# A hybrid decoder step: residual rows kept in SBUF, stores on ScalarE's queue, another order of work from up to down and at the end

## The chip, the core and the metric

The kernel runs on one core of one Trainium2 chip. TensorE (PE) multiplies, VectorE (DVE), ScalarE (ACT) and GpSimd (POOL) do the elementwise work, and SyncE (SP) issues most of the DMAs. The metric is the device time of one execution in microseconds (us), as the median of several runs.

## What is computed

One layer of a decoder: a norm, one input projection, sliding-window attention beside gated linear attention (GLA), an output projection with a residual add, a second norm, and a SwiGLU feed-forward block with a residual add. There are 1024 prompt rows and 16 meta tokens with model width 1024, and 8 x 8 sample rows; the feed-forward width is 2816, that is 11 pairs of 128 columns. Everything is in float32.

```python
def merge_heads(a, o_gla, og, gla_norm, w_o):
    g = rms_norm(o_gla.astype(a.dtype), gla_norm) * jax.nn.silu(og.reshape(b, t, GLA_HEADS, GLA_DV))
    merged = jnp.concatenate([a, g.reshape(b, t, GLA_V_W)], axis=-1)
    return jnp.einsum('bte,ed->btd', merged, w_o)

def swiglu(h, w_gate, w_up, w_down):
    u = jax.nn.silu(jnp.einsum('btd,df->btf', h, w_gate)) * jnp.einsum('btd,df->btf', h, w_up)
    return jnp.einsum('btf,fd->btd', u, w_down)
...
        x = x + merge_heads(a, o, og, gla_norm[l], w_o[l])
        x = x + swiglu(rms_norm(x, norm2[l]), w_gate[l], w_up[l], w_down[l])
```

## The kernel before

**Number format.** A float32 operand is split into a rounded part "hi" (ACT cast, L1218 or L99) and a rest "lo" (DVE subtract, L1219 or L100). A product is three matmuls, hi by hi, hi by lo and lo by hi (mm3, L105 to L107). For the sample rows the moving operand holds hi and lo side by side, so two matmuls do (mm2, L111 and L112).

**Order of the work.** The order on PE is the program's: generators that yield their estimated cost are interleaved by `merge` (L978), and after that the code is plain loops. ACT, DVE, POOL and SP get their order from a tile scheduler; each of them runs its list strictly in that order, and an instruction that waits holds up everything behind it on the same engine. DMA issues stand in those lists too.

**Up to the second norm.** `merge` at L1092 interleaves the GLA chunks, the attention, the projections and `out0`, which holds out_proj(0) and out_proj(1). out_proj(g) multiplies three row tiles by w_o (L105 to L107, tile `pw`), adds the product to the residual rows `xr` (L1072) and writes them to DRAM as x1d (L1074, on POOL's DMA queue). A second `merge` interleaves out_proj(2) with `norms_a`, which normalises tiles -1 (sample rows) to 3: it loads the rows back from x1d (L1168, on SP), squares and scales them (ACT, L1145 and L1147), turns them on PE (L1155, tile `tp`) and evacuates them (L1157). Only the tiles of the last out_proj stay in SBUF (`x1t`).

**Gate and up.** For each of the 11 pairs p the products with w_gate and w_up are computed with seven block products instead of eight (a Strassen/Winograd form, ORDER = 1, 2, 6, 7, 5, 4, 3). A block product is 24 matmuls of 544 columns in two parts and has a PSUM tile `pf`, of which there are four; the first product of a set is copied out by ACT (L1263), the others are added by DVE (L1265 to L1276). `blocks_A` loads weights on SP, forms block sums on POOL (L1236 to L1239) and splits them into hi_wg, lo_wg, hi_wu, lo_wu. What I call the tail of a pair follows: DVE multiplies up by the silu of gate (L1335), POOL forms block sums (L1346 to L1351), ACT and DVE split the result into `uo`, and SP stores it to DRAM: four small stores usd (L1336) and seven large ones ud (L1343).

**Down.** The pairs are taken in chunks (0), (1, 2), ..., (9, 10). For each chunk the weights are loaded, combined on POOL (L1393 to L1396) and split (`blocks_W`, tiles hi_wd, lo_wd); the sample rows `u8` are loaded and split (u8hl) and multiplied; then for each of four row pairs tp the tile `u` is loaded back from ud (L1406, on SP) and seven products are made into `pd`, of which there are eight PSUM buffers. In the first chunk a product is evacuated into an accumulator Y, by an ACT copy or by a DVE add of the residual, which is loaded again from x1d (L1448, L1450); in later ones DVE adds it (L1470). The last chunk combines the seven accumulators of a row pair while its products arrive (L1474 to L1489, DVE and POOL) and stores the output from SP (L1479, L1490, L1492, L1494).

## Time and profile before

| what | value |
|---|---|
| median of 3 runs | 1297.12 us (1296.54 to 1298.06) |
| the profiled execution: its own time | 1292.29 us |
| its span in the trace | 1290.5 us |
| mean granted TensorE clock | 0.97 of full speed |
| PE busy | 1201.3 us, 93% |
| DVE, ACT, POOL busy | 897.4, 526.8, 412.8 us |

Every time below is from the profiled execution, with 0 at the start of its span. A row of the timeline reads: start, duration, engine, line, operation, output tile <- input tiles, shape, count, and in brackets how long the engine had sat idle before it and what released it. Consecutive instructions of one kind may share a row; its duration then runs from the first start to the last end. "SPq" is the issue of a DMA by SP, not its transfer. A row of the stretches reads: from and to, length, then for PE, weight loads, DVE, ACT and POOL the busy time and the number of instructions, then the granted TensorE clock (1.00 is 2.4 GHz, 0.50 is 1.2 GHz), the share of the DMA engines and GB/s. Matmuls are pipelined, so one that shows 0.39 us is followed by the next after less.

### The profile page before, as it was taken

The page shows a single profiled execution, that of the slowest core. Times are in us where ns is not written, and L with a number is a line of the kernel's source. Part 1 is how long each engine was busy: PE and PEld are TensorE (multiplying, and loading weights), DVE is VectorE, ACT ScalarE, POOL GpSimd, SP SyncE. Part 2 cuts the span into 40 slices and gives each one's busy share as a digit, 9 for nine tenths or more (in the row PEclk, how much of TensorE's full clock was granted, in tenths as well). Part 3 has the DMA queues.
Part 4 walks back from the last instruction along what each step waited for, and adds up shares of the span by engine and source line. Part 5 has one row for each costly group of instructions (what it writes and reads, how often), then busy time and mean ns, then how long its engine had stood idle before and what let it go on. Part 6 is the DMA issues. An engine that isn't in the chain of part 4 may idle for free. (4 is left out here: it accounts for less than half of the span.)

```text
span 1290.5 us, 23115 instructions
## 1 busy us (share of the span) xinstructions
PE 1201.3 (93%) x9106; PEld 1060.6 (82%) x9106; DVE 897.4 (70%) x1758; ACT 526.8 (41%) x938; POOL 412.8 (32%) x354
## 2 busy tenths in 40 slices
PE   6999899999999969799999999999999479999997
PEld 6878787788767857699999999999999458788785
DVE  6747986887599648746665666576657656776687
ACT  5635665664566246523333333343324241221120
POOL 6202202131020111234543454345435422420445
PEclk9989999999999979899999999999999789999999
DMA  6723422243322753215433543354344594665545
GB/s 189 221 76 96 127 79 76 54 120 99 98 82 82 278 200 99 66 51 181 133 117 117 180 133 114 120 176 138 108 125 154 171 357 176 232 246 192 218 175 208
DMA packets 146986, 189.19 MB, mean 147 GB/s; under 512 B 15755, under 2 KB 114990, under 8 KB 146862
## 3 DMA queue, kind: packets, MB, share of 16 engines
q1 hardware_dynamic: 145038, 180.84, 43.1%
q0 software_dynamic: 1840, 6.88, 1.5%
q8 instruction: 71, 1.16, 0.4%
q14 instruction: 37, 0.30, 0.1%
HBM read 136.31 MB, written 52.43 MB: 146 GB/s over the span
## 5 line engine op out<-in xcount | busy, mean ns | idle before, releaser
L105 PE MATMUL pd<-hi_wd,u 128*128 128x512 f32 x308 | 121.9, 396 | 14.0 <-DMA u<-ud 13.8
L106 PE MATMUL pd<-lo_wd,u 128*128 128x512 f32 x308 | 121.6, 395 | 1.5 <-DVE lo_wd L1219 1.5
L107 PE MATMUL pd<-hi_wd,u 128*128 128x512 f32 x308 | 122.0, 396 | 0.0
L1218 ACT CAST hi_wd<-raw_wd 128x1024 fp32r<-128x1024 f32 x44 | 44.9, 1049 | 145.5 <-PE pd L107 75.5
L1470 DVE TENSOR_TENSOR y<-y,pd 128x512 f32<-128x512 f32 x112 | 75.3, 684 | 40.3 <-PE pd L107 40.1
L1218 ACT CAST hi_wg<-raw_wg 128x1024 fp32r<-128x1024 f32 (+1 forms) x44 | 41.5, 943 | 150.7 <-PE pf L106 68.3
L1219 DVE TENSOR_TENSOR uo<-u,uo 128x512 fp32r<-128x512 f32 x77 | 79.6, 1046 | 20.2 <-ACT uo L1218 18.8
L1219 DVE TENSOR_TENSOR lo_wu<-raw_wu,hi_wu 128x1024 fp32r<-128x1024 f32 (+1 forms) x44 | 53.9, 1225 | 47.3 <-ACT hi_wu L1218 47.3
L105 PEld LDWEIGHTS pd<-hi_wd,u 128*128 128x128 f32 x308 | 58.5, 190 | 28.8 <-DMA u<-ud 15.2
L1218 ACT CAST hi_wu<-raw_wu 128x1024 fp32r<-128x1024 f32 (+1 forms) x44 | 41.5, 943 | 79.4 <-POOL raw_wu L1237 28.4
L1219 DVE TENSOR_TENSOR lo_wd<-raw_wd,hi_wd 128x1024 fp32r<-128x1024 f32 x44 | 63.2, 1440 | 12.3 <-ACT hi_wd L1218 12.2
L106 PEld LDWEIGHTS pd<-lo_wd,u 128*128 128x128 f32 x308 | 58.5, 190 | 15.3 <-DVE lo_wd L1219 2.1
L1218 ACT CAST uo<-u 128x512 fp32r<-128x512 f32 x77 | 46.7, 620 | 56.4 <-POOL u L1346 40.1
L107 PEld LDWEIGHTS pd<-hi_wd,u 128*128 128x128 f32 x308 | 58.4, 190 | 12.4
L1219 DVE TENSOR_TENSOR lo_wg<-raw_wg,hi_wg 128x1024 fp32r<-128x1024 f32 (+1 forms) x44 | 49.1, 1116 | 24.9 <-ACT hi_wg L1218 24.9
L1236 POOL TENSOR_TENSOR raw_wg<-raw_wg 128x512 f32<-128x512 f32 x11 | 18.4, 1669 | 142.3 <-DVE lo_wg L1219 142.3
L590 POOL TENSOR_SCALAR sg<-sg 128x512 f32<-128x512 f32 (+1 forms) x9 | 14.1, 1564 | 134.0 <-ACT sg L589 133.9
L1393 POOL TENSOR_TENSOR raw_wd<-raw_wd 128x512 f32<-128x512 f32 x11 | 15.9, 1446 | 126.3 <-DVE lo_wd L1219 121.5
L106 PE MATMUL pw<-lo_wo,hThi 128*128 128x512 f32 x128 | 50.9, 397 | 3.2 <-DVE lo_wo L100 3.2
L105 PE MATMUL pw<-hi_wo,hThi 128*128 128x512 f32 x128 | 52.4, 410 | 0.3 <-DVE xr L1072 0.3
L107 PE MATMUL pw<-hi_wo,hTlo 128*128 128x512 f32 x128 | 50.5, 394 | 0.0
L1236 POOL TENSOR_TENSOR raw_wu<-raw_wu 128x512 f32<-128x512 f32 x11 | 14.2, 1294 | 88.5 <-DVE lo_wu L1219 88.5
(729 smaller groups left out, 4277.1 us busy)
## 6 DMA issues: line engine op xcount, KB each, us to landing
ud<-uo SPq DMA_DIRECT2D x77, 512.0 KB, 3.0
u<-ud SPq DMA_DIRECT2D x44, 896.0 KB, 6.1
raw_wo<-in_w_o_dram SPq DMA_DIRECT2D x24, 512.0 KB, 3.9
raw_wu<-in_w_up_dram SPq DMA_DIRECT2D x22, 512.0 KB, 3.9
raw_wg<-in_w_gate_dram SPq DMA_DIRECT2D x22, 512.0 KB, 4.2
raw_wd<-in_w_down_dram SPq DMA_DIRECT2D x22, 512.0 KB, 5.5
raw_q<-in_w_in_dram SPq DMA_DIRECT2D x12, 512.0 KB, 5.3
raw_gv<-in_w_in_dram SPq DMA_DIRECT2D x12, 512.0 KB, 3.6
```

Source lines behind the costliest of these rows:

```text
L105: nc.tensor.matmul(ps, lh, rh, start=first, stop=False)
L106: nc.tensor.matmul(ps, lh, rl, start=False, stop=False)
L107: nc.tensor.matmul(ps, ll, rh, start=False, stop=last)
L590: nc.gpsimd.tensor_scalar(s, s, 2.0 ** 60, None, op0=ALU.min)
L1218: nc.scalar.copy(hi, src)
L1219: nc.vector.tensor_tensor(lo, src, hi.bitcast(F32), op=ALU.subtract)
L1236: nc.gpsimd.tensor_tensor(a22, a21, a22, op=ALU.add)
L1393: nc.gpsimd.tensor_tensor(b11, b12, b11, op=ALU.subtract)
L1470: tt(a, a, ps, op=ALU.add)
```

## The change

It has three parts.

1. **Residual rows.** `x1t` now keeps every tile, so the second norm reads `xr` in SBUF and normalises it in place; the store to x1d stays, since the residual is read again in down. out_proj(1) moves out of the first merge into the second, where it runs before out_proj(2) (`out12`); norm2 of tiles 4 and 5 is issued earlier.
2. **Gate and up.** The weights of the next pair (for the last pair, the first chunk of down) are requested ahead of the tail, and the tail's eleven stores are issued by ACT instead of SP.
3. **Down.** `blocks_W` serves all pairs of a chunk in turn; the sample rows come after the products of the first chunk, or after the second row pair of later ones. The first chunk is evacuated by plain copies, alternately on ACT and DVE; the residual is added by POOL, one row pair in each of the four middle chunks (`residual`). The products come in the order 1, 2, 3, 7, 5, 6, 4. In the last chunk the accumulators of row pair 3 are combined before its products arrive, so that each product there needs few adds behind it, and the output is stored from ACT's queue.

```diff
             xr.append(x)
-            if g == NG - 1:
-                x1t[t] = x
+            x1t[t] = x
...
         yield from out_proj(0, xpool)
-        yield from out_proj(1, xpool)
...
-            x = x1t.get(t)
-            if x is None:
-                x = pool.tile([P, D], F32, tag="x", name=f"x1_{t}")
-                nc.sync.dma_start(x[0:64 if t < 0 else P], x1_rows(t))
+            x = x1t[t]
...
+    def out12():
+        for g in (1, 2):
+            yield from out_proj(g, npool)
+            traced.append(g)
...
-    merge(norms_a(), out_proj(2, npool))
+    merge(norms_a(), out12())
...
-            nc.sync.dma_start(usd[p][:, i // 2, i % 2, :], cu[i][:, 0:32])
+            nc.scalar.dma_start(usd[p][:, i // 2, i % 2, :], cu[i][:, 0:32])
...
-            nc.sync.dma_start(ud[p][:, :, ORDER.index(m)].rearrange("a p h t -> p a h t"), hl.bitcast(F32))
+            nc.scalar.dma_start(ud[p][:, :, ORDER.index(m)].rearrange("a p h t -> p a h t"), hl.bitcast(F32))
...
+    for p in range(NP):
+        if p:
+            full(A, cg)
+        A = blocks_A(w_up_v, p, "wu")
+        for a in cg:
+            nc.scalar.activation(a, a, AF.Silu)
+        cu = c_tiles(c2pool, "u")
+        full(A, cu)
+        now = cu, cg
+        if p < NP - 1:
+            cg = c_tiles(c1pool, "g")
+            A = blocks_A(w_gate_v, p + 1, "wg")
+        else:
+            W = blocks_W((0,))
+        tail(p, *now)
...
+    def residual(tp):
...
+        ts(y[2], y[2], x1[:, D1], op=ALU.add)
+        ts(y[3], y[3], x1[:, D2], op=ALU.add)
+        ts(y[4], y[4], x2, op=ALU.subtract)
...
+    def finish_combined(tp, m, ps):
...
+        elif m == 4:
+            tt(y[4], y[4], ps, op=ALU.subtract)
+            nc.scalar.dma_start(yp[rows(t2), D1], y[4])
+        elif m == 3:
+            tt(y[3], y[3], ps, op=ALU.add)
+            nc.scalar.dma_start(yp[rows(t1), D2], y[3])
...
+    DOWN = (1, 2, 3, 7, 5, 6, 4)
...
+        if c:
+            W = blocks_W(pairs)
         for tp in range(4):
             U = [load_u(p, tp) for p in pairs]
...
+            for j, m in enumerate(ORDER if last and tp == 3 else DOWN):
...
                 if first:
-
-                    if m == 2:
-                        tt(a, x[0][:, D1], ps, op=ALU.add)
...
+                    if j % 2:
+                        nc.vector.tensor_copy(a, ps)
                     else:
                         nc.scalar.copy(a, ps)
...
+            if c - 1 == tp and not last:
+                residual(tp)
+            if tp == (3 if first else 1):
+                samples(pairs, first, last)
```

How the order moves at the three places that the prediction speaks of:

**PE, last GLA chunk.** Before: `psn` is the state update of the chunk, `pw` the output projection, `tg` the transposes of the normed GLA output `on`; between `psn` and `tg` stand 48 matmuls of `pw`, of which the first three and the last three are shown.

```order
L777 MATMUL po_gla<-S,qG 128x256
L780 MATMUL po_gla<-gv,AT 128x128 x2
L786 MATMUL psn<-gv,kdT 64x128 x4
L105 MATMUL pw_5478<-hi_wo,hThi 128x512
L106 MATMUL pw_5478<-lo_wo,hThi 128x512
L107 MATMUL pw_5478<-hi_wo,hTlo 128x512
...
L105 MATMUL pw_5479<-hi_wo,hThi 128x512
L106 MATMUL pw_5479<-lo_wo,hThi 128x512
L107 MATMUL pw_5479<-hi_wo,hTlo 128x512
L674 MATMUL tg<-ident,on 128x128 x4
```

The same place with the change:

```order
L777 MATMUL po_gla<-S,qG 128x256
L780 MATMUL po_gla<-gv,AT 128x128 x2
L786 MATMUL psn<-gv,kdT 64x128 x4
L674 MATMUL tg<-ident,on 128x128 x4
L105 MATMUL pw_5561<-hi_wo,hThi 128x512
L106 MATMUL pw_5561<-lo_wo,hThi 128x512
L107 MATMUL pw_5561<-hi_wo,hTlo 128x512
```

The 48 matmuls between `psn` and `tg` have moved behind `tg`, into the second merge.

**DVE, end of the up products of a pair.** Before: L1276 is the last add of the up products, L1335 the multiply with silu(gate), `uo` the split of the tail, `lo_wg` the rest part of the next gate weights.

```order
L1276 TENSOR_TENSOR u_10727<-u_10727,pf_10911 128x544
L1219 TENSOR_TENSOR uo<-u_10729,uo 128x4x128
L1335 TENSOR_TENSOR u_10727<-u_10727,g_10512 128x544
L1219 TENSOR_TENSOR lo_wg<-raw_wg,hi_wg 128x1024
L1219 TENSOR_TENSOR uo<-u_10729,uo 128x4x128
```

The same place with the change:

```order
L1279 TENSOR_TENSOR u_10735<-u_10735,pf_10895 128x544
L1222 TENSOR_TENSOR uo<-u_10737,uo 128x4x128
L1222 TENSOR_TENSOR lo_wg<-raw_wg,hi_wg 128x1024
L1333 TENSOR_TENSOR u_10735<-u_10735,g_10456 128x544
L1222 TENSOR_TENSOR uo<-u_10737,uo 128x4x128
```

`lo_wg` now stands ahead of the last multiply.

**SP and ACT, from up to down.** SP before: usd and ud are the stores of the last pair, the loads of `u` for the first chunk of down (L1406) come behind them, each with loads of the residual.

```order
L1343 DMA ud_6164<-uo 128x4x256
L1336 DMA usd_6175<-u_11193 128x32
L1343 DMA ud_6164<-uo 128x4x256 x5
L1406 DMA u<-ud_6154 128x1792
L1448 DMA x_11544<-x1d_108 128x1024
L1450 DMA x1h<-x1d_109 128x512
L1406 DMA u<-ud_6154 128x1792
```

SP with the change:

```order
L83 DMA raw_wu<-in_w_up_dram 128x8x128 x2
L83 DMA raw_wd<-in_w_down_dram 128x1024 x3
L1420 DMA u<-ud_6147 128x1792 x4
L1426 DMA u_11653<-usd_6158 128x128
L83 DMA raw_wd<-in_w_down_dram 128x1024 x3
```

ACT with the change, at the same place (L1555 is the copy of a first-chunk product from PSUM):

```order
L1340 DMA ud_6157<-uo 128x4x256 x2
L1221 CAST uo<-u_11200 128x4x128
L1221 CAST uo<-u_11202 128x4x128
L1340 DMA ud_6157<-uo 128x4x256 x2
L1221 CAST u8hl<-u_11653 128x2x64
L1221 CAST hi_wd<-raw_wd 128x1024 x2
L1555 COPY y_1_11477<-pd 128x512
L1555 COPY y_3_11483<-pd 128x512
```

On SP the four loads of `u` are no longer behind any store; on ACT the first copy out of PSUM is now behind all the casts and stores of the last tail.

## Rows read from the trace of the kernel before

**Rows 1.** The page, part 1: busy time of each engine.

```profile
PE 1201.3 (93%) x9106; PEld 1060.6 (82%) x9106; DVE 897.4 (70%) x1758; ACT 526.8 (41%) x938; POOL 412.8 (32%) x354
```

**Rows 2.** Stretches: before the gate, the steady part, and at the start of down.

```profile
460.00:500.00 40.00, 29.17 (x139) 24.34 (x138) 24.52 (x44) 25.27 (x41) 6.51 (x15) 0.83 0.52 173
...
560.00:1000.00 440.00, 433.87 (x3418) 431.14 (x3417) 286.12 (x337) 153.56 (x214) 200.26 (x123) 1.00 0.44 135
...
1020.00:1040.00 20.00, 8.90 (x28) 7.04 (x28) 7.62 (x9) 4.49 (x9) 3.22 (x2) 0.66 0.83 307
```

**Rows 3.** Timeline, PE: where waits before the gate ended.

```profile
476.57 1.11 PE L1155 MATMUL tp<-ident,x_-1_5759 64*128 64x64 f32 x8 [8.69 <-ACT x_-1_5759 L1147]
...
479.83 3.68 PE L1155 MATMUL tp<-ident,x 128*128 128x128 f32 x16 [2.15 <-ACT x L1147]
...
508.20 0.80 PE L106 MATMUL pw<-lo_wo,hThi 128*128 128x512 f32 x1 [3.15 <-DVE lo_wo L100]
```

**Rows 4.** Timeline, ACT: the first square of the second norm.

```profile
473.25 1.06 ACT L1145 ACTIVATE junk_-1_5761<-x_-1_5759 64x1024 bf16<-64x1024 f32 x1 [8.83 <-DMA x_-1_5759<-x1d-1_107]
```

**Rows 5.** Timeline, DVE: an earlier GLA chunk, from state update to normed output.

```profile
373.65 1.43 DVE L792 SCALAR_TENSOR_TENSOR S<-S,eG,psn 64x128 f32<-64x128 f32 x4
...
375.71 0.68 DVE L666 TENSOR_REDUCE ms<-on 128x4 f32<-128x512 f32 x1
...
378.40 1.13 DVE L669 SCALAR_TENSOR_TENSOR on<-po_gla,r,sg 128x128 f32<-128x128 f32 x4 [1.21 <-POOL r L165]
```

**Rows 6.** Timeline, SP, PE and ACT: one pair of the steady part.

```profile
927.95 0.37 SPq L1343 DMA_DIRECT2D ud<-uo  x1
...
930.98 0.40 PE L107 MATMUL pf<-T2hia,lo_wg 128*128 128x288 f32 x1 [0.54 <-DVE lo_wg L1219]
...
932.63 0.61 ACT L1263 COPY g<-pf 128x544 f32<-128x544 f32 x1
...
936.87 0.30 PE L105 MATMUL pf<-T1hia,hi_wg 128*128 128x288 f32 x1
```

**Rows 7.** Timeline, PE: the waits between up and the first chunk of down.

```profile
1016.60 0.77 PE L111 MATMUL pd<-hi_wd,u8hl 128*128 128x512 f32 x1 [6.12 <-DVE u8hl L1219]
...
1031.22 0.79 PE L105 MATMUL pd<-hi_wd,u 128*128 128x512 f32 x1 [11.10 <-DMA u<-ud]
```

**Rows 8.** Timeline, POOL, ACT and SP: the tail of the last pair.

```profile
1019.43 2.12 POOL L1351 TENSOR_TENSOR u<-u,u 128x512 f32<-128x512 f32 x1
...
1021.58 0.62 ACT L1218 CAST uo<-u 128x512 fp32r<-128x512 f32 x1 [1.58 <-POOL u L1351]
...
1023.79 0.97 SPq L1343 DMA_DIRECT2D ud<-uo  x2
...
1024.86 0.99 SPq L1406 DMA_DIRECT2D u<-ud  x1
```

**Rows 9.** Timeline, PE: the waits for the sample rows of the second chunk.

```profile
1058.54 0.80 PE L111 MATMUL pd<-hi_wd,u8hl 128*128 128x512 f32 x1 [5.24 <-DVE u8hl L1219]
...
1064.27 0.80 PE L111 MATMUL pd<-hi_wd,u8hl 128*128 128x512 f32 x1 [3.65 <-DVE u8hl L1219]
```

**Rows 10.** Timeline, PE and SP: the last chunk, to the last store.

```profile
1263.78 0.50 PE L105 MATMUL pd<-hi_wd,u 128*128 128x512 f32 x1 [1.50 <-DMA u<-ud]
...
1274.89 0.51 PE L105 MATMUL pd<-hi_wd,u 128*128 128x512 f32 x1 [1.21 <-DMA u<-ud]
...
1283.72 0.40 PE L107 MATMUL pd<-hi_wd,u 128*128 128x512 f32 x1
...
1287.11 0.41 SPq L1494 DMA_DIRECT2D out_dram<-y  x1
```

**Rows 11.** The page, parts 5 and 6: splits, accumulations and transfers of down.

```profile
L1218 ACT CAST hi_wd<-raw_wd 128x1024 fp32r<-128x1024 f32 x44 | 44.9, 1049 | 145.5 <-PE pd L107 75.5
L1470 DVE TENSOR_TENSOR y<-y,pd 128x512 f32<-128x512 f32 x112 | 75.3, 684 | 40.3 <-PE pd L107 40.1
...
u<-ud SPq DMA_DIRECT2D x44, 896.0 KB, 6.1
```

More of the change, by code (lines that the diff above doesn't have):

```diff
@@ L1127, in hymba_step @@
     c1pool_, c1pool = open_pool("c1", 5, "right")
-    npool_, npool = open_pool("n", 4, "right")
-    napool_, napool = open_pool("na", 4)
+    npool_, npool = open_pool("n", 6, "right")
     def h2_part(m, sl, src):
@@ L1291, in norms_b @@
     def norms_b():
-        xt = [normed2(tp, npool) for tp in (2, 3)]
+        norm2(5, x1t[5], npool)
+        xt = [[(t, x1t[t]) for t in (4, 5)], normed2(3, npool)]
         yield 0.0, 4.0
@@ L1323, in full, with tail @@
             combine(t, slice(0, NH), m, ps[2])
-    for p in range(NP):
-        if p:
-            cg = c_tiles(c1pool, "g")
-            full(blocks_A(w_gate_v, p, "wg"), cg)
-        for a in cg:
-            nc.scalar.activation(a, a, AF.Silu)
-        cu = c_tiles(c2pool, "u")
-        full(blocks_A(w_up_v, p, "wu"), cu)
+    def tail(p, cu, cg):
         tt, ts = nc.vector.tensor_tensor, nc.gpsimd.tensor_tensor
@@ L1352, in hymba_step, with blocks_W, put @@
         put(6, a11), put(3, a12)
+    def blocks_W(pairs):
+        W = [{} for p in pairs]
+        raws = [[load_raw([w_down_v[:, f:f + 1, :]], 1, D, "wd") for f in (2 * p, 2 * p + 1)] for p in pairs]
+        def put(i, j, n):
+            for B, raw in zip(W, raws):
+                hl = parts("wd")
+                split_into(*hl, raw[n])
+                for c, m in enumerate((i, j)):
+                    B[m] = tuple(a[:, c * 512:c * 512 + 512] for a in hl)
+        put(1, 0, 0)
+        put(2, 3, 1)
+        for raw in raws:
+            (b11, b12), (b21, b22) = (halves(r) for r in raw)
+            nc.gpsimd.tensor_tensor(b11, b12, b11, op=ALU.subtract)
+            nc.gpsimd.tensor_tensor(b12, b22, b12, op=ALU.subtract)
+            nc.gpsimd.tensor_tensor(b22, b22, b11, op=ALU.subtract)
+            nc.gpsimd.tensor_tensor(b21, b22, b21, op=ALU.subtract)
+        put(5, 7, 0)
+        put(4, 6, 1)
+        return W
+    for p in range(NP):
[13 more added lines that the diff above has]
+        tail(p, *now)
     psp_.__exit__(None, None, None)
@@ L1368, in hymba_step @@
     wpool.append(w2)
+    nsplit[0] = 4
     upool = last_pool("u", 4, "right")
@@ L1417, in hymba_step, with rows, samples @@
     CHUNKS = [(0,)] + [(p, p + 1) for p in range(1, NP, 2)]
-    tt = nc.vector.tensor_tensor
-    for pairs in CHUNKS:
-        first, last = pairs is CHUNKS[0], pairs is CHUNKS[-1]
-        W = [blocks_W(p) for p in pairs]
+    tt, ts = nc.vector.tensor_tensor, nc.gpsimd.tensor_tensor
+    def rows(t):
+        return slice(t * P, t * P + P)
+    def samples(pairs, first, last):
         US = [load_u8(p) for p in pairs]
-        if first:
-            x8 = xpool2.tile([P, D], F32, tag="x", name="x8")
-            nc.sync.dma_start(x8[0:64], x1_rows(-1))
         for half, blocks in ((D1, (1, 2)), (D2, (0, 3))):
@@ L1432, in hymba_step @@
             if first:
-                tt(Y8[0:64, half], x8[0:64, half], ps[0:64], op=ALU.add)
-                nc.scalar.copy(Y8[64:128, half], ps[64:128])
+                nc.scalar.copy(Y8[:, half], ps)
             else:
@@ new lines, in finish @@
+    def finish(tp, x22, m, ps):
+        y = Y[tp]
+        t1, t2 = 2 * tp, 2 * tp + 1
+        a = y[m]
+        if m != 4:
+            tt(a, a, ps, op=ALU.add)
+        if m == 2:
+            ts(a, a, y[1], op=ALU.add)
+            nc.scalar.dma_start(yp[rows(t1), D1], a)
+        elif m == 7:
+            ts(x22, x22, a, op=ALU.add)
+            ts(y[4], a, y[4], op=ALU.subtract)
+        elif m == 6:
+            tt(a, a, y[1], op=ALU.add)
+            tt(y[1], a, y[5], op=ALU.add)
+            ts(x22, x22, y[1], op=ALU.add)
+            nc.scalar.dma_start(yp[rows(t2), D2], x22)
+            tt(y[3], y[3], y[1], op=ALU.add)
+            nc.scalar.dma_start(yp[rows(t1), D2], y[3])
+        elif m == 4:
+            tt(a, a, ps, op=ALU.subtract)
+            tt(a, a, y[6], op=ALU.add)
+            nc.scalar.dma_start(yp[rows(t2), D1], a)
@@ L1442, in hymba_step @@
+    DOWN = (1, 2, 3, 7, 5, 6, 4)
+    NC = len(CHUNKS)
+    for c, pairs in enumerate(CHUNKS):
+        first, last = c == 0, c == NC - 1
+        if c:
+            W = blocks_W(pairs)
         for tp in range(4):
             U = [load_u(p, tp) for p in pairs]
-            y = Y[tp]
-            t1, t2 = 2 * tp, 2 * tp + 1
-            if first:
-                x = [xpool2.tile([P, D], F32, tag="x", name="x1")]
-                nc.sync.dma_start(x[0], x1_rows(t1))
-                x.append(xpool2.tile([P, 512], F32, tag="xh", name="x1h"))
-                nc.sync.dma_start(x[1], x1_rows(t2)[:, D1])
```

115 lines of the change are left out of this document (56 added, 59 removed).

## The prediction, as put on record before the run

> **What bounds the kernel now.** I read the page first: PE is busy for 1201.3 of 1290.5 us [rows 1], so no change of order can take off more than about 89 us, and only where PE stands still or runs slowly. The view of stretches shows where that is. From 560 to 1000 PE is busy for 433.87 of 440 us at full clock; from 460 to 500 for only 29.17 of 40 us, and from 1020 to 1040 for 8.90 of 20 us with a granted clock of 0.66, that is, partly at 1.2 GHz [rows 2]. Then I read PE's timeline for its idle brackets. Three groups stand out: before the gate 8.69, 2.15 and 3.15 us [rows 3], from up to down 6.12 and 11.10 [rows 7] and again 5.24 and 3.65 [rows 9], and at the end 1.50 and 1.21 [rows 10]. In the steady part there is one wait of 0.54 us a pair for lo_wg [rows 6]; ten pairs have it. The change touches all four places, so I cost it place by place, by what PE waits for there now and will wait for next.
>
> **The price of a matmul.** From 1274.89 to 1283.72 PE starts 38 matmuls after the wait for the second tile `u` (row pair 3 has 42, and three come before it) [rows 10]: 0.232 us each, so a single-pair product of three is 0.70 and the first chunk with its 28 products 19.5 us. After a long wait they go slower. The eight sample matmuls from 1016.60 until the next wait begins (1031.22 - 11.10 = 1020.12) take 3.52 us [rows 7] instead of 1.86, a loss of 1.7. The first chunk takes from 1031.22 to 1058.54 - 5.24 = 1053.30 [rows 7, 9], 22.1 us instead of 19.5, a loss of 2.6. Those are my prices for a restart of PE.
>
> **Place 1, before the gate.** The reload of x1 goes, and with it the 8.83 us for which ACT's first square waits on that DMA [rows 4], seen on PE as 8.69 and then 2.15. The 3.15 for lo_wo should go too, since its split is no longer late behind the norm. With a restart of 1.8 (between 1.7 and 2.6, by the shorter wait) that is 15.8 us. What is late next: in the last GLA chunk the 48 matmuls between `psn` and `tg` no longer cover the chain that makes `on`. In an earlier chunk that chain runs on DVE from the state update at 373.65 to the last multiply at 378.40 + 1.13 [rows 5], 5.9 us with other work of up to 0.7 in it. I take 5.4 as PE's new wait. Then three row tiles are normed on ACT before PE can turn the third: one square and one scale more than is covered, about 1.06 each by the square's row [rows 4], 2.2 together. The second long wait again costs a restart, 2.2. Sum of the new: 9.8. **Gain 6.** Bounds: 0, if the third tile's norm and the restart are twice that dear, and 12, if PE's remaining `pw` cover the norms and there is no second restart.
>
> **Place 2, the steady part.** On DVE lo_wg moves ahead of one multiply of about 0.7 us (the DVE add of the same kind is 0.68 [rows 11]), so the 0.54 can vanish ten times: 5.4 us. Against that ACT issues eleven stores a pair, 0.37 us each by SP's row [rows 6], 4.1 us of a pair of 43.2 us. By its total ACT has room: it is busy for 153.56 of 440 us [rows 2]. But an issue waits for DVE's split, and what is queued behind it on ACT is the copy of g that frees the first of four `pf` tiles. That copy now ends at 932.63 + 0.61 = 933.24, and PE's fifth product starts at 936.87 [rows 6], a slack of 3.6 us. Behind two more casts of 0.62 [rows 8] and two or three issues with their waits I place its end between 934.7 and 936.4. It still makes it, narrowly, so I take **a gain of 3**, with bounds of 5.4 and, if each pair loses 0.5 net, -5. The earlier requests for weights cost nothing: SP's stores that stood among them are gone.
>
> **Place 3, from up to down.** The sample rows and the loads of `u` cause all four waits: 6.12 + 11.10 + 5.24 + 3.65 = 26.1 us [rows 7, 9]. The load of `u` is issued at 1024.86 because it stands on SP behind the last stores, whose final issue ends at 1023.79 + 0.97; that store waits for POOL's block sum, which ends at 1021.55, and for the splits behind it [rows 8]. With the change the loads stand before any of this, and the sample rows come after the products. With the restarts 1.7 and 2.6, and for the second pair of waits 1.15 (1058.54 to 1060.62 for four matmuls) and an estimate of 1.5, the full worth is 33 us. What is late next: PE can now run the first chunk from 1010.5 on, but has eight `pd` buffers. Eight products end at about 1016.1. The ninth needs the first copy by ACT, which stands behind the whole last tail: the last cast `uo` ends at 1022.2 [rows 8], the last two issues after DVE's splits at about 1024.8, and then come a small cast and two of 1.05 [rows 11], so the copy ends at about 1027.5. PE waits 11 us and pays a restart of 2. ACT then serves products and weight splits in turn, and the raw weights of the second chunk arrive late as their buffers come free; I take 2 for that. **Gain 33 - 11 - 2 - 2 = 18.** Bounds: 31, if ACT does not hold PE up, and 10, if a whole load (6.1 by that of `u` [rows 11]) and a POOL sum of about 2 [rows 8] stand uncovered ahead of the second chunk, 8 more.
>
> **The middle chunks.** The residual is added by three POOL instructions a chunk, at most 2.12 each by the nearest POOL row [rows 8], in a stretch of some 38 us; the next accumulation into the same tiles comes a chunk later. The cover is POOL's idle two thirds [rows 1]; if it were gone, 3 x 2.1 us in four chunks would be at stake. I count nothing.
>
> **Place 4, the end.** The loads of `u` no longer stand behind output stores on SP, so 1.50 + 1.21 = 2.7 go. The last matmul ends at 1283.72 + 0.40 = 1284.1 and the span at 1290.5, 6.4 us later, of which 1290.5 - 1287.52 = 3.0 follow the last issue [rows 10]. With the change one add of 0.68 [rows 11], one issue of 0.41 and the 3.0 follow: 4.1. **Gain 2.7 + 2.3 = 5**, bounds 2 and 6.
>
> **The sum.** 6 + 3 + 18 + 5 = 32 us off the profiled execution's 1292.3: 1260.3. The median of the runs stands 4.8 above that execution, so I forecast **1265 us**.
>
> **Rivals.**
>
> *ACT is in time at the start of down.* If the tail's stores and casts are spread early enough, the ninth product does not wait, and place 3 is worth 31: a sum of 45, 1247.3 + 4.8 = **1252**. For it: ACT is busy only a third of the time [rows 2]. Against it: the last cast of the tail cannot start before POOL's sum at 1021.55 [rows 8], and the first copy stands behind it. Chance 0.18.
>
> *The transfers, not their place in the queue, set when `u` arrives.* From 1020 to 1040 the DMA engines already move 307 GB/s at a share of 0.83 [rows 2]. If stores on ACT's queue, weight loads and the `u` loads share them so that PE's first product still starts near 1031, place 3 is worth the 5.24 and 3.65 with their restarts and little else, 11, and place 4 keeps its two waits, worth 2. The sum is then 6 + 3 + 11 + 2 = 22: 1270.3 + 4.8 = **1275**. Against it: the load stands behind a waiting store in time, not in bandwidth; it is issued right after that store [rows 8]. Chance 0.12. The Trainium skill, in "DMA: Bandwidth & Descriptors", section "Issuing engines are not separate DMA queues", states the rule behind this rival: starting DMAs on several engines saves only the sequencer's time for the start, since all run on the same engines. By that rule alone the move of the stores would be worth their issue time. The trace disagrees for this place, with SP's issues waiting until 1024.76 for POOL and DVE.
>
> *ACT holds up every pair (slower).* If the copy of g slips not to 936.4 but past 940.2, that is by 3.6 + 3.3 us from where it ends now, PE loses 3.3 us in each of ten pairs, 33 in all. The other places give 29, so the time is 1292.3 + 4 + 4.8 = **1301**. The price per pair from which this decides is 3.2 us, since under that the sum is still a gain within the measurement. For it: the stores' waits for DVE lie on the engine that frees PSUM. Against it: ACT's busy third. Chance 0.05.
>
> *Nothing comes of it:* the gains of places 1 and 3 are given back in full, by waits of the same length; chance 0.03.
>
> **Chances and range.** The forecast has 0.62, the rivals 0.18, 0.12, 0.05 and 0.03. About 0.2% of the time, 2.6 us, is what a measurement can tell from no change. Faster by more: 0.62 + 0.18 + 0.12 = 0.92; same 0.03; slower 0.05. The forecast's own range, by the bounds of place 3 and half those of the others, is 1253 to 1277. The range for 8 in 10 takes in the first two rivals with their own spread: 1247 to 1286.
>
> **What would show it.** Right: no wait for a DMA of x1 on ACT before the gate, but one of 4 to 7 us on PE for `tg` or `on`; no 0.54 waits for lo_wg; PE's first product of down near 1010 on the old clock, then, eight products later, one wait of 8 to 13 us that ends with ACT's first copy of y; no waits of several us for u8hl; 3 to 5 us from the last matmul to the end. Wrong: a wait on PE for a `pf` tile in every pair; a first product of down that waits for `u`; or a second chunk that waits more than 4 us for its weights.

## The result and the profile after

| | before | changed |
|---|---|---|
| median of the runs | 1296.83 us (4 runs) | 1278.10 us (4 runs) |
| ratio, 95% interval | | 0.986 [0.9843, 0.9878] |
| profiled execution, its span | 1292.29, 1290.5 us | 1279.4, 1277.6 us |

The change made the kernel 1.4% faster, 18.7 us by the medians; the forecast was 1265, the range 1247 to 1286. The two profiled executions are only 12.9 us apart, because that of before lies below its other runs and that of the change above its own. The working was made against profiled executions, so it is held against those 12.9. (In the experiments below the median of the kernel before is 1292 to 1294 us, so the 18.7 may be some 2 to 5 us too many.)

The page and the stretches of the changed kernel, to be read beside [rows 1, 2]:

```profile
PE 1197.0 (94%) x9106; PEld 1058.5 (83%) x9106; DVE 887.7 (69%) x1756; ACT 525.5 (41%) x939; POOL 433.3 (34%) x371
```

```profile
460.00:500.00 40.00, 38.37 (x170) 31.82 (x171) 24.86 (x30) 21.45 (x27) 4.10 (x9) 0.96 0.49 172
560.00:1000.00 440.00, 436.49 (x3431) 433.11 (x3431) 282.37 (x337) 151.80 (x214) 192.78 (x123) 1.00 0.44 136
1020.00:1040.00 20.00, 6.30 (x13) 4.11 (x14) 9.13 (x12) 8.20 (x13) 7.99 (x6) 0.50 0.89 318
```

PE is now busy for 38.37 of the 40 us from 460 to 500, where it was 29.17. From 1020 to 1040 it is busy for less than before, 6.30 against 8.90 us, at a granted clock of 0.50, that is at 1.2 GHz for the whole stretch.

Because the absolute times shift, I cut each trace at five points of PE's timeline: the last `psn`, the first gate product, the first up product, the last up product, the last matmul, and the end of the span. The lengths of these stages, worked out from the starts of those matmuls, are the table in which all kernels of this study stand:

| kernel | psn to gate | to first up | gate and up | to last matmul | to the end | ratio to before [95%] |
|---|---|---|---|---|---|---|
| before | 87.9 | 38.5 | 454.0 | 273.5 | 6.8 | |
| changed | 82.9 | 42.0 | 452.4 | 255.9 | 13.4 | 0.9860 [0.9843, 0.9878] |
| e1 tail stores on SP | 81.5 | 41.7 | 447.7 | 252.2 | 13.5 | 0.9801 [0.9774, 0.9828] |
| e2 samples early | 81.4 | 42.0 | 452.2 | 258.3 | 11.6 | 0.9862 [0.9836, 0.9889] |
| e3 last tail on DVE | 82.8 | 43.4 | 452.1 | 255.3 | 13.5 | 0.9881 [0.9853, 0.9909] |
| e4 x1 store on SP | 82.9 | 38.7 | 450.5 | 254.9 | 13.3 | 0.9832 [0.9803, 0.9860] |
| e5 last stores on ACT | 81.4 | 41.8 | 447.7 | 255.8 | 13.4 | 0.9836 [0.9812, 0.9860] |
| e6 old finish | 82.7 | 42.4 | 451.0 | 265.8 | 9.6 | 0.9889 [0.9865, 0.9913] |
| e7 no residency | 88.6 | 38.7 | 451.9 | 256.2 | 13.1 | 0.9885 [0.9859, 0.9910] |
| e8 combined | 82.6 | 36.5 | 447.7 | 258.5 | 9.5 | 0.9773 [0.9748, 0.9798] |
| e9 combine ahead | 82.6 | 42.1 | 453.0 | 269.3 | 4.8 | 0.9896 [0.9875, 0.9916] |
| e10 u ahead | 82.9 | 42.1 | 447.7 | 249.3 | 13.4 | 0.9787 [0.9767, 0.9808] |
| e11 best | 82.8 | 36.6 | 447.7 | 262.8 | 4.7 | 0.9765 [0.9742, 0.9789] |
| e12 combine one | 82.1 | 37.8 | 447.7 | 253.1 | 6.9 | 0.9737 [0.9713, 0.9761] |

Before against changed: +5.0, -3.5, +1.6, +17.6 and -6.6 us, together 14.2 before rounding. The part ahead of `psn`, which the change does not touch, was 1.3 longer; in the study's traces it lies between 426.7 and 431.1 us. That makes the 12.9. (Untouched stages also differ by a few tenths to 1.5 us between kernels; I read nothing from such differences.)

Where PE waits now, from its timeline (start, duration, what; in brackets the idle time and what ended it):

```profile
437.35 1.16 PE L674 MATMUL tg<-ident,on 128*128 128x128 f32 x4 [5.66 <-DVE on L669]
...
528.29 1.94 PE L1150 MATMUL tp<-ident,xr 128*128 128x128 f32 x8 [7.04 <-DVE xr L1152]
...
606.82 0.40 PE L107 MATMUL pf<-T2hia,lo_wu 128*128 128x288 f32 x1 [0.73 <-DVE lo_wu L1222]
...
1029.49 0.79 PE L105 MATMUL pd<-hi_wd,u 128*128 128x512 f32 x1 [14.74 <-ACT y L1555]
...
1033.65 0.79 PE L105 MATMUL pd<-hi_wd,u 128*128 128x512 f32 x1 [2.51 <-DVE y L1553]
...
1036.99 0.80 PE L105 MATMUL pd<-hi_wd,u 128*128 128x512 f32 x1 [1.70 <-ACT y L1555]
```

These answer to [rows 3, 6, 7, 9, 10]. The reload is gone, and in its place stand the chain of the GLA output (5.66) and a wait of 7.04 inside the gate. The 0.54 for lo_wg is gone, and in six of the ten pairs after the first there is one of 0.18 to 0.73 for lo_wu, which makes 2.8 us. Down starts without a wait for `u`, makes eight products, and then waits 14.74 us for ACT's first copy. After 1037 there is no wait over 0.6 us left, none for u8hl and none for `u` at the end.

ACT, SP and DVE from up to down, which answer to [rows 8]:

```profile
1007.12 1.27 SPq L1420 DMA_DIRECT2D u<-ud  x3
...
1014.68 0.62 ACT L1221 CAST uo<-u 128x512 fp32r<-128x512 f32 x1 [4.77 <-POOL u L1343]
...
1018.98 0.62 ACT L1221 CAST uo<-u 128x512 fp32r<-128x512 f32 x1 [3.68 <-DMA ud<-uo]
...
1023.79 0.62 ACT L1221 CAST uo<-u 128x512 fp32r<-128x512 f32 x1 [2.36 <-DMA ud<-uo]
1023.81 1.71 ACTq L1340 DMA_DIRECT2D ud<-uo  x2
...
1028.86 0.58 ACT L1555 COPY y<-pd 128x512 f32<-128x512 f32 x1
...
1032.90 1.89 DVE L1553 COPY y<-pd 128x512 f32<-128x512 f32 x3 [3.64 <-DMA ud<-uo]
...
1036.35 2.05 ACT L1555 COPY y<-pd 128x512 f32<-128x512 f32 x4 [6.92 <-DMA ud<-uo]
```

The loads of `u` go out at 1007, as the order promised. But twice a cast of the last tail waits for a landed store, since there are three `uo` buffers, and the copy that PE needs stands behind all of it. The next copies out of PSUM wait for landed stores again; the last store of `uo` goes out at 1025.16 and lands at 1036.28. A copy does not read `uo`, so it must be the accumulator it writes that is not free: the source closes the pool of `uo` before it allocates the accumulators, and I infer that they share memory. These waits are PE's 2.51 and 1.70.

The last chunk, DVE, POOL, PE and ACT, which answers to the second half of [rows 10]:

```profile
1256.57 5.67 DVE L1483 TENSOR_TENSOR y<-y,y 128x512 f32<-128x512 f32 x1
...
1261.65 1.74 POOL L1481 TENSOR_TENSOR y<-y,y 128x512 f32<-128x512 f32 x1
...
1263.43 0.69 DVE L1490 TENSOR_TENSOR y<-y,pd 128x512 f32<-128x512 f32 x1 [1.19 <-POOL y L1481]
...
1264.18 0.40 PE L107 MATMUL pd<-hi_wd,u 128*128 128x512 f32 x1
...
1266.91 0.67 DVE L1511 TENSOR_TENSOR y<-y,pd 128x512 f32<-128x512 f32 x1
...
1274.32 0.34 ACTq L1531 DMA_DIRECT2D out_dram<-y  x1
```

PE's last matmul starts at 1264.18, but DVE only begins on the first product of row pair 3 (L1511) at 1266.91. All seven are then waiting in PSUM, and the end is DVE's and POOL's: 13.4 us against 6.8 before.

### The profile page after: what moved, and what is told of

Read it like the earlier page. It is cut to its first block, busy times and chain, and to the rows that moved or that the text cites. A ratio compares the mean times of both kernels' runs of the same rounds, so it can differ in the third digit from the quotient of the medians.

```text
span 1277.6 us, 23094 instructions
## 1 busy us (share of the span) xinstructions
PE 1197.0 (94%) x9106; PEld 1058.5 (83%) x9106; DVE 887.7 (69%) x1756; ACT 525.5 (41%) x939; POOL 433.3 (34%) x371
## 3 DMA queue, kind: packets, MB, share of 16 engines
q10 hardware_dynamic: 49376, 45.56, 11.1%
## 4 chain that ended last, share of the span: by engine, by line
PE 36%; issue 25%; POOL 17%; DVE 13%; ACT 4%; DMA 4%; POOLq 0%; SPq 0%; DVEq 0%; ACTq 0%
PE pd L105 4%; PE pd L106 4%; PE pd L107 4%; DMA ud<-uo 2%; POOL raw_wu L1242 2%; ACT hi_wg L1221 2%; POOL raw_wg L1240 1%; POOL raw_wg L1239 1%; PE gv L105 1%; PE gv L107 1%; PE gv L106 1%; POOL u L1348 1%; POOL u L1346 1%; PE q L105 1%; PE q L107 1%
## 5 line engine op out<-in xcount | busy, mean ns | idle before, releaser
L1222 DVE TENSOR_TENSOR lo_wu<-raw_wu,hi_wu 128x1024 fp32r<-128x1024 f32 (+1 forms) x44 | 49.2, 1118 | 55.5 <-ACT hi_wu L1221 55.5
L105 PEld LDWEIGHTS pd<-hi_wd,u 128*128 128x128 f32 x308 | 58.4, 190 | 34.0 <-ACT y L1555 17.6
L106 PEld LDWEIGHTS pd<-lo_wd,u 128*128 128x128 f32 x308 | 58.5, 190 | 13.5 <-DVE lo_wd L1222 0.8
L1369 POOL TENSOR_TENSOR raw_wd<-raw_wd 128x512 f32<-128x512 f32 x11 | 18.9, 1717 | 70.7 <-DVE lo_wd L1222 70.7
```

The source lines that it names most:

```text
L105: nc.tensor.matmul(ps, lh, rh, start=first, stop=False)
L106: nc.tensor.matmul(ps, lh, rl, start=False, stop=False)
L1222: nc.vector.tensor_tensor(lo, src, hi.bitcast(F32), op=ALU.subtract)
L1369: nc.gpsimd.tensor_tensor(b22, b22, b11, op=ALU.subtract)
```

## The experiments

All were timed in five rounds against the kernel before, whose median was 1292 to 1294 us in these; so the ratios are what is compared. That median was 1296.83 us in the runs beside the changed kernel, a difference of 0.004, so a ratio nearer than that to the changed kernel's 0.9860 (e2 to e7 and e9) says little by itself; there the stages decide. e1 to e7 and e9 change one thing of the changed kernel; e8 and e10 to e12 join several.

**e1: the tail's stores back on SP.**

```diff
-            nc.scalar.dma_start(usd[p][:, i // 2, i % 2, :], cu[i][:, 0:32])
+            nc.sync.dma_start(usd[p][:, i // 2, i % 2, :], cu[i][:, 0:32])
...
-            nc.scalar.dma_start(ud[p][:, :, ORDER.index(m)].rearrange("a p h t -> p a h t"), hl.bitcast(F32))
+            nc.sync.dma_start(ud[p][:, :, ORDER.index(m)].rearrange("a p h t -> p a h t"), hl.bitcast(F32))
```

> Undoes one part: the tail's eleven stores a pair are issued by SP again, all else as in the changed kernel. In SP's list one load of u for the first chunk then stands ahead of the last six stores, three behind them. Theory (a waiting issue on ACT holds up what stands behind it): the waits for lo_wu at the up products, six pairs of ten with 0.28 to 0.73 us, 3.3 in all, go; the first ACT copy of down comes 1 to 3 us earlier than 1028.86, and PE's first wait in down ends at 1026 to 1031, now by the late loads of u. Sum -4 to +2 us. Rival (the place of the loads behind the stores is the whole worth of the part): PE's second row pair waits for u until after 1031 and the kernel is 5 us or more slower.

Measured: 0.9801, below the changed kernel's interval, 7.6 us faster by the ratios, where -4 to +2 was expected. Gate and up take 447.7 us instead of 452.4, flat over all pairs; the waits for lo_wu are gone but for the one at the first pair. The stage to the last matmul is 3.7 shorter, although PE now waits for `u`. The timeline of ACT, SP and PE in e1:

```profile
1011.60 0.62 ACT L1221 CAST uo<-u 128x512 fp32r<-128x512 f32 x1 [2.72 <-POOL u L1348]
1012.12 0.58 ACT L1555 COPY y<-pd 128x512 f32<-128x512 f32 x1
...
1013.42 1.99 SPq L1420 DMA_DIRECT2D u<-ud  x3
...
1019.65 0.79 PE L105 MATMUL pd<-hi_wd,u 128*128 128x512 f32 x1 [13.80 <-DMA u<-ud]
```

The last up product starts at 997.93 in this run, so the first copy comes 14.2 us after it, where it took 1028.86 - 1008.24 = 20.6 with the stores on ACT. So the expected gain was too small: moving the stores to ACT's queue cost more than it gave. The rival, 5 us or more slower, falls.

**e5: only the last pair's stores on ACT.** The two lines of e1, with `nc.sync if p < NP - 1 else nc.scalar`.

> The stores of the pairs 0 to 9 go back to SP, those of the last pair stay on ACT. Theory (two separate losses on ACT's queue: one in every pair, one from up to down): the stretch of gate and up shrinks as it did with all stores on SP, 452.4 to about 447.7 us, and the start of down stays as in the changed kernel with a wait of some 14 us for ACT's first copy and 255 us from the last up product to the last matmul; in all 4 to 5 us faster than the changed kernel, 3 to 4 slower than with all stores on SP. Rival (the place of the last stores decides nothing): as fast as with all stores on SP, within 1.5 us.

Measured: 0.9836; gate and up 447.7 as in e1, to the last matmul 255.8 as in the changed kernel, with waits of 14.38 and 4.58 us. There are two losses and they are separate, 4.7 in the pairs and 3.6 from up to down; the gain on the changed kernel, some 3 us, is a little less than the 4 to 5 expected.

**e3: the last tail's block sums on DVE.** `ts = tt if p == NP - 1 else nc.gpsimd.tensor_tensor`.

> For the last pair alone the four block sums of the tail run on DVE instead of POOL. Theory (the first copy out of PSUM is late because the tail's chain POOL, ACT, DVE, store is long): the four sums take 4 x 0.7 instead of 5.7 us, the wait of 14.74 us on PE at the start of down shrinks by 3 to 5, and so does the time. Rival (the casts wait for landed stores of uo, of which there are three buffers): the wait shrinks by less than 1.5 us.

Measured: 0.9881, no gain; the waits are 14.29 and 4.73. POOL's sums are not what the copy waits for, so the rival stands: the casts wait for landed stores, 4.39 and 2.52 us in this trace.

**e4: the x1d stores of out_proj(2) on SP.**

```diff
-            nc.gpsimd.dma_start(x1_rows(t), xr[i][0:64 if t < 0 else P])
+            (nc.sync if g == 2 else nc.gpsimd).dma_start(x1_rows(t), xr[i][0:64 if t < 0 else P])
```

> The x1d stores of out_proj(2) are issued by SP instead of POOL, where they stand behind block sums. Theory (normalising in place has to wait until the store of the same tile has landed): ACT's wait of 4.57 us for x1d ahead of the scaling goes to under 1, PE's wait of 7.04 us at 521 falls to 2 to 4, the time by 3 to 5. Rival (the chain square, POOL's root, scaling is the bound there): PE waits 6 to 7 us as before, under 1 us in the time.

Measured: 0.9832, and the stage from the first gate to the first up product falls from 42.0 to 38.7. In the changed kernel ACT's scaling waits for the store of the tile that it overwrites. Behind it on ACT stands a copy of g, behind that copy on DVE an add and then the evacuation of `tp`, and for that PE waits:

```profile
524.03 1.15 ACT L1142 ACTIVATE xr<-xr,r 128x1024 f32<-128x1024 f32 x1 [4.57 <-DMA x1d<-xr]
```

With the stores on SP that wait is gone from ACT and PE's 7.04 has become 2.34:

```profile
521.88 1.15 ACT L1142 ACTIVATE xr<-xr,r 128x1024 f32<-128x1024 f32 x1 [0.66 <-POOL r L165]
523.01 1.16 PE L1150 MATMUL tp<-ident,xr 128*128 128x128 f32 x8 [2.34 <-DVE xr L1152]
```

**e7: part 1 undone,** with the code of the kernel before for it.

> Undoes part 1: out_proj(1) back in the first merge, tiles -1 to 4 loaded again from DRAM ahead of the second norm, as in the kernel before; the rest as changed. Theory (part 1 took 10.8 us of waits for the reload away and gave most of it back to the wait for the GLA chain, 5.7 us, and to the third tile's norm behind its own store, 7.0): the time rises by only 1 to 3 us. Rival (part 1 is worth the 6 us that the prediction gave it): it rises by 5 to 7.

Measured: 0.9885. The first two stages take 127.3 instead of 124.8 us, with PE's old waits back (9.29, 2.15 and 2.97). Part 1 is worth 2.5 us by the traces, as the theory said; by the ratios the two kernels' intervals overlap.

**e2: the samples of the last chunk earlier.** `if tp == (3 if first else 0 if last else 1)`.

> In the last chunk the sample rows come after row pair 0 instead of 1, so POOL's two sums for them (2.4 us each) leave the stretch ahead of the finish of row pair 2. Theory (POOL's order at the end is what makes DVE late): the 13.4 us from the last matmul to the end of the span become 8 to 10, the kernel 3 to 5 us faster. Rival (DVE has too much to do in the last chunk, whatever the order): under 1 us.

Measured: 0.9862, no change. The end is 1.8 shorter and the stage ahead of it 2.4 longer. The place of POOL's sample sums in the chunk is not the cause.

**e6: the old finish for row pairs 0 to 2,** with the code of the kernel before in `finish` and ORDER in the whole last chunk.

> In the last chunk row pairs 0 to 2 are finished as in the kernel before (product order 1, 2, 6, 7, 5, 4, 3, its adds and its POOL sums); row pair 3 and the queues stay as changed. The number of adds is the same. Theory (with the new order the add that frees a PSUM buffer stands on DVE behind POOL's sums of the same row pair, and DVE falls behind PE): the 13.4 us from the last matmul to the end fall to 5 to 8, the time by 5 to 8. Rival (DVE has simply too many adds in this chunk, whatever their order): 11 to 14 us remain.

Measured: 0.9889. The end falls to 9.6, but the last matmul comes 9.9 later. The theory about the order falls: in this place the old finish is no better. Of the delay 5.9 us lie in the last chunk, which takes 48.9 us instead of 43.0, with waits of 2.83 and 0.68 us for hi_wd and lo_wd at its head and a granted clock of 0.81 from 1230 to 1240. Most of the rest lies in the four chunks before, which the edit does not touch: without a wait each takes 42.9 us instead of 42.1, and why is not shown.

**e8: e1, e4 and e6 together.**

> A candidate better than both kernels: the changed kernel with the tail's stores on SP, the x1d stores of out_proj(2) on SP, and the old finish of row pairs 0 to 2 in the last chunk. If the three gains are separate they add: 7.6 for the tail's stores, 3.6 for the x1d stores and 5 to 8 for the end, 16 to 19 us faster than the changed kernel, a ratio to the kernel before of 0.971 to 0.974. If the end is bound by DVE whatever the order: 11, a ratio of 0.977.

Measured: 0.9773, the value named for an end that DVE bounds. The end is 4.0 us shorter than in e1 and the stage ahead of it 6.3 longer, so the gain is that of e1 and e4, and the finish adds nothing.

**e9: all row pairs combined in the fifth chunk.** The last chunk uses ORDER and `finish_combined` for every row pair.

```diff
+            if c == NC - 2:
+                x22 = xpool2.tile([P, 512], F32, tag="xh", name="x22")
+                nc.sync.dma_start(x22, x1_rows(2 * tp + 1)[:, D2])
+                combined(tp, x22)
```

> The accumulators of all four row pairs are combined in the fifth chunk, not those of row pair 3 alone in the last: three adds of two SBUF tiles on DVE and one POOL sum of each of row pairs 0 to 2 leave the last chunk, and every add of DVE that is left there reads PSUM. Theory (in the last chunk DVE's adds of two SBUF tiles, 0.7 us alone and 1.2 to 5.7 beside POOL, and its waits for POOL make it fall behind PE): the 13.4 us from the last matmul to the end become 4 to 6, the last matmul comes at most 2 later, the time falls by 6 to 9. Rival (the added work in the fifth chunk holds up PE there by as much): within 2.

Measured: 0.9896, and by the stages 4.8 us slower than the changed kernel. The end does become short, 4.8 us, now that every product's add of DVE in the last chunk reads PSUM; but the edit moves sums of POOL as well, so which of the two makes it short stays open. What it costs is that the sums hold up the last chunk's weights, as PE's timeline of e9 shows:

```profile
1227.51 0.59 PE L105 MATMUL pd<-hi_wd,u 128*128 128x512 f32 x1 [4.34 <-ACT hi_wd L1221]
...
1230.87 0.79 PE L106 MATMUL pd<-lo_wd,u 128*128 128x512 f32 x1 [2.76 <-DVE lo_wd L1222]
```

With two more of 0.99 and 0.89 that is 9.0 us, and the clock in the stretch from 1220 to 1240 is 0.74. ACT's casts hi_wd wait there for POOL's sums of the weights, and POOL runs without a pause from 1212.21 to 1238. The theory was right for the end alone: the last matmul comes 13.4 us later, not 2. The rival named the right cost and put it too low, since the loss is larger than the gain.

**e10: `u` ahead of the stores.** e1, and

```diff
+        dma = nc.scalar if (p, tp) == (0, 1) else nc.sync
-        nc.sync.dma_start(u.bitcast(F32), ud[p][tp])
+        dma.dma_start(u.bitcast(F32), ud[p][tp])
```

> As with all tail stores on SP, and the load of u of the first chunk's second row pair is issued by ACT, so that in SP's list three loads of u stand ahead of the last six large stores. Theory (with the stores on SP the start of down waits for u alone, since ACT's first copy is done by 1012.7 on that run's clock and u lands at 1019.6): the wait of 13.8 us falls to 7 to 9, the time by 4 to 6 against that run, a ratio to before of about 0.976. Rival (the loads take the DMA engines from the last stores, whose buffers the tail waits for): the wait ends with ACT's copy and stays above 11.

Measured: 0.9787; the wait falls from 13.80 to 7.34 us and the stage by 2.9. The wait now ends with ACT's copy, as the rival said, though well under 11 us, and PE's first product waits 3.08 us for hi_wd, where in e1 it waited 2.58 for `u`. By the ratio it can't be told from e1.

**e11: e1, e4, e9 and e10 together.**

> The changes that helped together: tail stores and the x1d stores of out_proj(2) on SP, the loads of u ahead, all row pairs combined in the fifth chunk. If they add up: 7.6 + 3.6 + 5 + 7 = 23 us faster than the changed kernel, a ratio to before of 0.968. If the end or the start of down is bound elsewhere: 0.973 to 0.978.

Measured: 0.9765: short end (4.7), late weights (8.5 us of waits at the head of the last chunk), as in e9.

**e12: as e11, but only row pair 0 combined ahead;** row pairs 1 and 2 as changed, row pair 3 in the last chunk.

> Tail stores and x1d stores of out_proj(2) on SP, u ahead, and only row pair 0 is combined in the fifth chunk; row pairs 1 and 2 are finished as in the changed kernel, row pair 3 combined in the last chunk. Theory (POOL and DVE have room for one row pair's sums in the fifth chunk, where four held up the last weights by 9 us): PE's waits at the head of the last chunk stay under 2 us, the end after the last matmul falls from 13.4 to 8 to 11, ratio to before 0.972 to 0.975. Rival (each row pair combined ahead costs as much there as it saves at the end): ratio 0.976 to 0.979, as with the kernels on these parts alone.

Measured: 0.9737 [0.9713, 0.9761], 1259.08 us beside 1292.37 before: faster than both kernels. The head of the last chunk costs one wait, more than the 2 us expected, and the end is shorter than expected, 6.9:

```profile
1208.56 0.79 PE L105 MATMUL pd<-hi_wd,u 128*128 128x512 f32 x1 [2.82 <-ACT hi_wd L1221]
...
1250.43 0.40 PE L107 MATMUL pd<-hi_wd,u 128*128 128x512 f32 x1
...
1254.22 0.34 ACTq L1532 DMA_DIRECT2D out_dram<-y  x1
```

The short end is not the gain. The last chunk takes 48.6 us here and 43.1 in e10, so the chunk and the end together take 55.5 against 56.5: by these traces combining row pair 0 ahead is worth about 1 us, and most of what leaves the end comes back ahead of the last matmul, as the rival said. The rest is e1, e4 and e10 joined, which was not run without the combining.

## Why the prediction was right or wrong

The sign and the range of 1247 to 1286 were right, and so was what PE waits for first in the main stage. The sum of 32 us was not: by the stages it is 14.2. The median of 1278.10 lies just outside the forecast's own range of 1253 to 1277, and as a number the second rival's 1275 came nearer, though not by its mechanism. Every place gave less than was forecast, and that the miss is not larger is luck: 5.1 us came from the middle chunks, which the prediction counted at nothing.

**Place 1, forecast 6, measured 1.6,** that is 5.0 ahead of the gate and -3.5 inside the first gate. The reload's waits went, and the chain that makes `on` cost 5.66 against the 5.4 worked out. Ahead of the gate PE waited for no norm, and 1.97 of the 3.15 for lo_wo stayed. The step that failed is "three row tiles are normed on ACT before PE can turn the third ... 2.2 together": it ends at the gate, has no term for the norms inside it, and no thought for the store. A tile that is normalised in place can't be overwritten until its x1d store has landed, and those stores stand on POOL among the block sums of the first gate weights. The wait was 7.04 us on PE, in the gate, and e4 shows that the store was the cause of 4.7 of it. It was there before too, as 1.06 us on ACT. I had looked at what the change adds, not at what the moved work now stands next to.

**Place 2, forecast 3, measured 1.6.** The 0.54 for lo_wg went, as the order said, and the copy of g did make it. The loss came elsewhere, in the split of the up weights, for which the working has no term. One pair of the changed kernel:

```profile
588.64 2.07 ACTq L1340 DMA_DIRECT2D ud<-uo  x2
590.80 0.62 ACT L1221 CAST uo<-u 128x512 fp32r<-128x512 f32 x1 [1.58 <-DVE uo L1222]
592.54 0.62 ACT L1221 CAST uo<-u 128x512 fp32r<-128x512 f32 x1 [1.11 <-DMA ud<-uo]
...
593.06 1.05 ACT L1221 CAST hi_wu<-raw_wu 128x1024 fp32r<-128x1024 f32 x1
...
598.14 1.29 POOL L1239 TENSOR_TENSOR raw_wu<-raw_wu 128x512 f32<-128x512 f32 x1 [6.67 <-DVE lo_wu L1222]
...
599.60 0.30 PE L105 MATMUL pf<-B11hia,hi_wu 128*128 128x288 f32 x1
...
600.83 1.05 ACT L1221 CAST hi_wu<-raw_wu 128x1024 fp32r<-128x1024 f32 x1 [2.68 <-POOL raw_wu L1240]
```

The same pair of e1, with the stores on SP:

```profile
582.98 1.05 ACT L1221 CAST hi_wu<-raw_wu 128x1024 fp32r<-128x1024 f32 x1
...
591.51 1.29 POOL L1239 TENSOR_TENSOR raw_wu<-raw_wu 128x512 f32<-128x512 f32 x1 [5.69 <-DVE lo_wu L1222]
...
593.96 0.30 PE L105 MATMUL pf<-B11hia,hi_wu 128*128 128x288 f32 x1
...
594.21 1.05 ACT L1221 CAST hi_wu<-raw_wu 128x1024 fp32r<-128x1024 f32 x1 [2.69 <-POOL raw_wu L1240]
```

With the stores on ACT the first hi_wu is cast 6.5 us ahead of the first up product (599.60 - 593.06), with the stores on SP 11.0 us ahead (593.96 - 582.98): in ACT's list it stands behind two more casts of the tail and behind issues that wait for DVE's splits. From there the delay runs on through DVE's lo_wu and POOL's sum to the cast at 600.83, for which ACT itself is idle. That cast starts 1.23 us after the first up product, in e1 0.25, and PE then waits 0.73 us for lo_wu. The ten up products after the first take up to 22.2 us each in the changed kernel, 21.2 in e1; that is the whole loss. With the stores on SP the part is worth 6.3 us; the move to ACT's queue took 4.7 of it. The slower rival had the right kind of mechanism, on another tile and a seventh of its size.

**Place 3, forecast 18, measured 10.3.** The stage of 17.6 us in the table holds more than this place. From the last up product to the end of the second chunk, and from there to the last chunk, first before, then changed:

```profile
1010.20:1107.06 96.86, 70.75 (x279) 56.32 (x278) 61.39 (x73) 30.57 (x45) 26.51 (x18) 0.84 0.72 260
1107.06:1238.54 131.48, 128.06 (x553) 103.27 (x552) 93.67 (x120) 25.61 (x30) 39.67 (x27) 1.00 0.57 210
```

```profile
1008.24:1094.78 86.54, 67.18 (x279) 53.32 (x278) 54.90 (x70) 29.62 (x46) 33.08 (x24) 0.88 0.72 251
1094.78:1221.13 126.35, 126.35 (x553) 103.67 (x552) 91.00 (x120) 25.84 (x29) 47.22 (x31) 1.00 0.64 236
```

Eight products, then a wait for ACT's first copy: that was the forecast, with 11 us. It was 14.74. I let the last cast follow POOL's sum, as in [rows 8]; with the change it waits for landed stores of `uo`, 3.68 and 2.36 us, and e3, which shortens POOL's part, gains nothing. In this stretch the loads of `u` and the weights share the DMA engines with those stores (share 0.89). The two terms of 2 us behind it were too small as well. At the pace of the three chunks that follow (126.35 us for the 552 matmuls that start there) the first two chunks need 63.2 us. Before, 33.7 us stood on top of that, as the prediction had it; with the change 23.4 do, where it took 11 + 2 + 2. They are the 14.74, the 2.51 and 1.70 for the next copies, and some 4.4 of slow matmuls and one short wait. The second chunk's weights, for which 2 us were set aside, were in time.

**The middle chunks, forecast 0, measured 5.1.** The residual cost PE nothing, as counted: in the third to fifth chunk it is busy for all of the 126.35 us. But before it had waited there for lo_wd, 0.76 us at 1115.97, 1.70 at 1196.52 and 0.76 at 1203.63, with slower matmuls after, and these waits went. Which part of the change removed them no run shows.

**Place 4, forecast +5, measured -4.5,** that is 2.1 in the last chunk and -6.6 behind it. The 2.7 for `u` went. The step that failed is "With the change one add of 0.68, one issue of 0.41 and the 3.0 follow": it takes for granted that DVE is level with PE at the last matmul. It was not. I had counted the adds behind the last matmul and not DVE's and POOL's work in the whole last chunk, where eight PSUM buffers let PE run on while DVE falls behind. From the first matmul of the last chunk to the end of the span, before and changed:

```profile
1238.54:1290.52 51.98, 42.86 (x185) 34.21 (x183) 41.79 (x51) 2.10 (x2) 26.51 (x18) 0.99 0.58 202
```

```profile
1221.13:1277.62 56.49, 42.83 (x185) 34.22 (x183) 45.08 (x52) 2.69 (x3) 40.25 (x25) 0.92 0.54 191
```

DVE has one instruction more, POOL seven: two sums of the residual that run over from the chunk before, two for the sample rows, and seven instead of four for row pair 3. DVE's adds of two SBUF tiles wait while POOL sums, as the last section shows. e2 and e6 show that the order inside the chunk is not the point; e9 shows that combining the accumulators ahead of the chunk brings the end to 4.8, near the 4.1 that the prediction worked out, and moves the cost to the weights ahead of it. By the last chunk and the end together no kernel gets back to the 52.0 us of before: it is 56.5 changed, 59.9 in e9 and 55.5 in e12. Which of POOL's sums costs how much no run separates.

**The rivals.** ACT was not in time, so the 1252 did not come. Of the transfers: in the changed kernel PE's first product did not wait for `u`, so that rival's mechanism fell for `u`. Something like it shows for the stores: they landed late behind the loads that now stand ahead of them (the last section), and the casts and copies waited for them. And the rule that stood beside it deserves more than I gave it. The Trainium skill ("DMA: Bandwidth & Descriptors", "Issuing engines are not separate DMA queues") says that starting DMAs on more engines saves only the time of starting them. e1 agrees: with the same loads and sums and the stores back on SP the kernel is faster (0.9801 against 0.9860). SP's wait until 1024.76, which the prediction held against the rule, does not bear on it: that was an issue waiting for POOL and DVE. So the gain of place 3 did not come from the queue of the stores. The three waits for u8hl, 15.0 us before, are gone in e1 too; how much the place of the sample rows, the plain copies and the order of the products bring each, no run separates.

Three sums of the prediction do not come out as written. By their own conditions the bounds of place 1 are 1.6 and 10.4, not 0 and 12. Its bounds of place 3 and half those of the others, added up, give 1247 to 1282 and not 1253 to 1277. And "nothing comes of it" still leaves the 8 us of places 2 and 4.

## What to carry to other kernels

A DMA issue that waits for another engine's result holds up every instruction behind it; an engine that splits weights or frees PSUM is a poor home for such stores, even at a third busy. Before a tail is shortened, compare each engine's work in the whole last stage with TensorE's, since PSUM buffers hide a lag until the last matmul. And when a tile is overwritten in place, look for the store that still reads it, and for the queue which that store stands in; the same goes for a buffer that takes the memory of an older one.

## What the runs showed of the hardware

DVE's add of two SBUF tiles waits while POOL sums, and an add that reads PSUM does not. From the changed kernel's timeline of DVE:

```profile
1239.10 1.19 DVE L1484 TENSOR_TENSOR y<-y,y 128x512 f32<-128x512 f32 x1
...
1246.20 0.76 DVE L1483 TENSOR_TENSOR y<-y,y 128x512 f32<-128x512 f32 x1
...
1248.76 0.68 DVE L1484 TENSOR_TENSOR y<-y,y 128x512 f32<-128x512 f32 x1
```

The same add takes 0.68 us with POOL idle, 1.19 at 1239.10 beside a sum on POOL, and the L1483 at 1256.57 shown above 5.67, while POOL ran five sums back to back; the adds with `pd` stay at 0.67 to 0.69 throughout. What counts is when POOL's sum ends: in this chunk every such add that begins during a POOL sum ends 0.55 us after the end of one. The add at 1246.20 took only 0.76 because POOL's sum, begun at 1245.12, ended at 1246.42. At 1256.57 the add missed three changes from one POOL sum to the next; why, the trace does not show. The Trainium skill ("GPSIMD Engine Reference", the table of specifications at its head) says that GpSimd shares its SBUF interface with VectorE, with contention for VectorE instructions with two SBUF inputs; the trace agrees. No run took the contention alone away, so how much of the 13.4 us it makes is open.

How long a store takes to land goes with what was requested ahead of it. In the changed kernel the stores of `uo` whose landing the trace has take 2.9 to 4.7 us from 560 to 1000. The last store, issued at 1025.16 behind a load of `u` (1024.20) and three loads of weights (from 1019.28 on), lands 11.1 us later. Before, the store issued at 1023.79, with the loads of `u` still behind it, lands 2.99 us later, though in that time the DMA engines have a share of 0.98:

```profile
1023.79:1026.78 2.99, 0.00 (x0) 0.00 (x0) 1.77 (x3) 1.16 (x2) 0.00 (x0) 0.50 0.98 319
```

So the share alone does not tell; no run changed the order of these requests and nothing else. The medians of the whole pages, 3.0 before and 3.8 with the change, rest on 11 and 10 landings, and I read nothing from them.
